# Neighbourhood attention and a feed-forward block: the feed-forward part's seams laid anew, with sums of the down weights kept in DRAM

## The chip, the cores and the metric

The kernel runs on one core of a Trainium2 chip. The metric is the device time of one execution in microseconds (us). A core has TensorE (PE; its weight loads are listed apart as PEld), VectorE (DVE), ScalarE (ACT), GpSimd (POOL) and SyncE (SP), each with its own stream of instructions that it takes in order, and 16 DMA engines, which take transfers from queues that SP, ACT and POOL fill. SBUF is the on-chip memory, PSUM the banks that TensorE writes, DRAM the memory off the core.

## The reference

The input is 1024 prompt rows and 512 sample rows of width 1024, in float32. The reference computes, for one layer:

```
x  = x + attention(rms_norm(x) * norm_mix) @ w_o       # 16 heads, a neighbourhood of rows, a bias table
h  = rms_norm(x) * norm_ffn
x  = x + (silu(h @ w_gate) * (h @ w_up)) @ w_down       # 1024 -> 2816 -> 1024
y  = rms_norm(x) * norm_final
```

All of it is in float32 precision: every matrix operand is split into a high part and the rest, and a product is three matmuls (high x high, high x rest, rest x high).

## The kernel before, in words

The attention part (up to L631) ends with the output projection: `project` (L578) takes an attention row tile and the weights `wo`, 12 matmuls 128x512 at a time into `pgo`, adds x and stores the sum to `x1_d` in DRAM. Only what follows is changed, apart from one early load.

**The operands.** The 1536 rows are worked in two chunks of 768 tokens, each cut into two halves of 384. Each matrix product of the feed-forward part is done on 2x2 blocks with seven products in place of eight (a Strassen-Winograd scheme). Its x side needs seven operands: three blocks and four sums. `norm2` (L658) loads an `x1_d` row tile, normalizes it (square with row sum on ACT, root on POOL, one scalar_tensor_tensor by root and gain on DVE), transposes it in eight 128x128 pieces on PE and copies these from PSUM. `pair` (L672) makes a tile's seven operands from two row tiles. Chunk 0's operands are split into SBUF tiles h0 to h6; chunk 1's go to `hop_d` in DRAM and are reloaded (L812) into the same seven tiles between the chunks. Both chunks' `pair`s stand ahead of the feed-forward part.

**Gate and up.** A chunk has 11 units (`unit`, L786) of 256 columns of the hidden 2816. A unit is a gate block and an up block, and a block (`blocks`) is seven products of 12 matmuls 128x384 into the banks pa, pb and pd. `w_ops` loads the block's two 512 KB halves of weights (`wr`), forms four sums of 128x512 on DVE (L741 to L746), and splits operands (L138 casts on ACT, L139 subtracts on DVE) into `wa` (a single one) and `ws` (two at once). Evacuations into `c` tiles, Silu on ACT, the gate's multiply on DVE, four sums on POOL (`gs`) and seven stores by POOL to `gop_d` follow.

**Down.** The seven operands n are run in the order 0, 1, 4, 5, 2, 6, 3. For each, `d_op` (L839) loads its 11 row pieces of w_d as 256 KB tiles `dr`, forms the sums on POOL (`tk`, L848, L851, L854, and L857) and splits them into `wd`; for each of six token tiles `g_op` (L862) loads 704 KB of `gop_d` into `gr`, splits it into `go`, and 33 matmuls 128x512 fill one of four banks. Additions to x (loaded again from `x1_d` on SP's queue) and, for the last row tiles, the final norm (`finish`, L879) follow each bank. The row tiles' y go out on SP's queue.

**Order.** A scheduler fixes each engine's stream when the kernel is built, from priorities and estimated times, so instructions of neighbouring steps may be interleaved other than written. A tile waits for its memory to be freed by its previous owner. Pools that are closed hand their memory to later ones.

Of the kernel before, what the change touches and what calls it, by code (L numbers as in the profile page):

```python
# [18 lines left out]
P = 128  # L19
D = 1024  # L20
# [35 lines left out]
def body(tc, xp, xs, g_mix, g_ffn, g_fin, w_qkv, rpb, w_o, w_g, w_u, w_d, yp, ys):  # L56
# [9 lines left out]
    with es:  # L66
# [16 lines left out]
        hop_d = dr.tile([7, P, KB // 2, HT], F32, name="hop_d")  # L83
        gop_d = dr.tile([7, 6, P, NP, P], F32, name="gop_d")


        ident = cpool.tile([P, P + 24], F32, name="ident")[:, :P]
# [4 lines left out]
        nc.gpsimd.memset(mhalf, -0.5)  # L92

# [539 lines left out]
        hop_cm, hop = pool("hop", bufs=1, reuse_waits="tile")  # L633

        def h_op(i):
            return hop.tile([P, 2, KB // 2, HT], F32R, tag=f"h{i}", name=f"h{i}")

        def operands(dst, xa, xb, tt):

            b11, b21, b12, b22 = xa[:, :4], xa[:, 4:], xb[:, :4], xb[:, 4:]  # L640
            t1, t2, t3, t4 = (tt[:, n] for n in range(4))
# [12 lines left out]
        n_cm, np_ = pool("npool", bufs=2, reuse_waits="tile")  # L654
        gb = np_.tile([P, D], F32, name="gbf", bufs=1)
        nc.sync.dma_start(out=gb, in_=bcast(g_ffn))

        def norm2(t):  # L658

            xn = np_.tile([P, D], F32, tag="xn", name="xn", bufs=3)  # L660
            nc.scalar.dma_start(out=xn, in_=x1_d[t * P:(t + 1) * P, :])
            xt = np_.tile([P, KB, P], F32, tag="xt", name="xt")
            rms(xn, gb, xn, xt.rearrange("p k t -> p (k t)"))
            for b in range(2):
                pt = psum("T", "pt")
# [3 lines left out]
                nc.scalar.copy(xt[:, b * 4:(b + 1) * 4], pt.rearrange("p (k t) -> p k t", k=4))  # L669
            return xt  # L670

        def pair(c, j, dst):  # L672
            xa = norm2(c * CT + j)
            xb = norm2(c * CT + 3 + j)
            tt = np_.tile([P, 4, KB // 2, P], F32, tag="tt", name="tt", bufs=1)
            operands(dst, xa, xb, tt)

        hops = [h_op(i) for i in range(7)]

        def to_sbuf(j):  # L680
            def dst(i, op):
                split(op, hops[i][:, 0, :, j * P:(j + 1) * P], hops[i][:, 1, :, j * P:(j + 1) * P])
            return dst

        def to_dram(j):
            def dst(i, op):
# [270 lines left out]
```

## Time and profile before

| what | us |
|---|---|
| three runs: lowest, median, highest | 1841.29, 1846.19, 1848.37 |
| the profiled execution's own time | 1845.18 |
| its span | 1843.4 |
| last output-projection matmul ends | 803.3 |
| last gate/up product ends | 1481.6 |
| last down matmul ends | 1835.1 |

The mean granted TensorE clock of the profiled execution is 0.985 of full speed. In the profile's rows a line such as L138 is that of the helper which recorded the operation (a split's cast), so tiles, not lines, tell the groups apart. "Idle before" names what ended an engine's idle time. The DMA share is the mean busy share of the 16 DMA engines.

### The profile page before, as it was taken

How to read it: one execution, taken by the hardware profiler on the slowest of the kernel's cores; microseconds unless marked ns; L12 is line 12 of the kernel's file. 1: busy time of each engine (PE TensorE's matmuls, PEld its weight loads, DVE VectorE, ACT ScalarE, POOL GpSimd, SP SyncE). 2: the span in 40 equal slices, each digit the busy share in tenths (PEclk: the TensorE clock that was granted, in tenths of full speed). 3: DMA queues.
4: the chain of work that ended last, by engine and by line, in shares of the span. 5: the costliest groups of instructions: out<-in, count | busy, mean ns of one | idle time of the engine just before them, and what ended most of it. 6: DMA issues, size and time to landing. Idle time of an engine off the chain costs nothing.

```text
span 1843.4 us, 25648 instructions
## 1 busy us (share of the span) xinstructions
PE 1754.1 (95%) x9178; PEld 1522.5 (83%) x9178; DVE 1192.9 (65%) x2191; ACT 863.7 (47%) x1706; POOL 448.4 (24%) x495
## 2 busy tenths in 40 slices
PE   8999999999999999979999999999999969999898
PEld 6877777777767777868999999899999958887676
DVE  4401877777896566768777777867777444545654
ACT  4411776766785554544443444444443333333322
POOL 1211000000130000112243342424243323526420
PEclk9999999999999999988999999999999979999999
DMA  7755334333464443676343434544333277635732
GB/s 245 221 183 160 111 105 113 108 101 103 126 208 146 133 149 100 221 247 185 108 121 118 133 110 151 164 129 125 108 120 107 68 272 245 225 130 191 232 129 100
DMA packets 222048, 278.80 MB, mean 151 GB/s; under 512 B 25600, under 2 KB 171776, under 8 KB 221920
## 3 DMA queue, kind: packets, MB, share of 16 engines
q1 hardware_dynamic: 201824, 210.69, 37.3%
q0 software_dynamic: 18368, 60.18, 9.5%
q10 hardware_dynamic: 1728, 6.29, 1.1%
q8 instruction: 72, 1.18, 0.3%
q14 instruction: 56, 0.46, 0.1%
HBM read 213.20 MB, written 76.43 MB: 157 GB/s over the span
## 4 chain that ended last, share of the span: by engine, by line
PE 68%; DVE 10%; DMA 9%; ACT 5%; issue 3%; SPq 2%; POOL 2%; DVEq 0%; ACTq 0%; POOLq 0%
PE pa L754 20%; PE pd L910 12%; PE pd L754 10%; PE pgv L278 7%; PE pg L332 6%; PE pb L754 5%; DMA vr<-v_d 5%; PE pgo L586 3%; DMA dr<-ffn_w_down 2%; PE pss L394 2%; PE ptt L420 2%; DVE pT L424 2%; SPq L378 2%; PE po L431 2%; ACT s L405 1%
## 5 line engine op out<-in xcount | busy, mean ns | idle before, releaser
L910 PE MATMUL pd<-wd,go 128*128 128x512 f32 x1386 | 323.0, 395 | 30.5 <-ACT go L138 20.4
L910 PEld LDWEIGHTS pd<-wd,go 128*128 128x128 f32 x1386 | 263.0, 191 | 90.4 <-ACT go L138 21.6
L754 PE MATMUL pa<-h,ws 128*128 128x384 f32 x1056 | 201.8, 339 | 2.9 <-ACT c L777 2.1
L754 PE MATMUL pa<-h,wa 128*128 128x384 f32 x1056 | 195.1, 338 | 7.0 <-ACT wa L138 4.5
L754 PE MATMUL pd<-h,ws 128*128 128x384 f32 x1056 | 198.3, 335 | 1.2 <-ACT h L138 0.6
L332 PE MATMUL pg<-hTp,whl 128*128 128x512 f32 x768 | 193.7, 399 | 0.0
L754 PEld LDWEIGHTS pa<-h,wa 128*128 128x128 f32 x1056 | 185.8, 190 | 8.9 <-ACT wa L138 5.2
L139 DVE TENSOR_TENSOR ws<-wt,ws 128x1024 fp32r<-128x1024 f32 x88 | 108.6, 1235 | 127.1 <-ACT ws L138 126.7
L754 PEld LDWEIGHTS pa<-h,ws 128*128 128x128 f32 x1056 | 185.1, 189 | 6.7 <-ACT c L777 4.3
L754 PEld LDWEIGHTS pd<-h,ws 128*128 128x128 f32 x1056 | 184.5, 188 | 1.8 <-ACT h L138 1.0
L332 PEld LDWEIGHTS pg<-hTp,whl 128*128 128x128 f32 x768 | 139.9, 188 | 27.5 <-issue 0.4
L805 POOL DMA_DIRECT2D gop_d<-c x66 | 50.5, 765 | 387.4 <-DVE c L796 380.3
L405 ACT ACTIVATE s<-s,mx 128x384 f32<-128x384 f32 (+1 forms) x192 | 110.7, 580 | 67.3 <-DVE mx L402 67.1
L586 PE MATMUL pgo<-wo,oh 128*128 128x512 f32 x576 | 139.3, 392 | 0.2 <-DVE oh L139 0.2
L139 DVE TENSOR_TENSOR wa<-wr,wa 128x512 fp32r<-128x512 f32 x132 | 117.8, 897 | 18.4 <-ACT wa L138 17.8
L138 ACT CAST ws<-wt 128x1024 fp32r<-128x1024 f32 x88 | 92.6, 1053 | 68.6 <-PE pd L754 65.4
L586 PEld LDWEIGHTS pgo<-wo,oh 128*128 128x128 f32 x576 | 105.6, 188 | 20.7 <-DVE oh L139 0.6
L138 ACT CAST go<-gr 128x1408 fp32r<-128x1408 f32 x42 | 57.7, 1374 | 131.2 <-PE pd L910 114.0
L138 ACT CAST wa<-wr 128x512 fp32r<-128x512 f32 x132 | 81.4, 621 | 62.8 <-PE pb L754 40.0
L754 PE MATMUL pb<-h,wa 128*128 128x384 f32 x528 | 102.0, 340 | 3.4 <-DVE c L774 3.4
L332 PE MATMUL pg<-hTs,whl 128*128 128x512 f32 x384 | 102.6, 404 | 0.8 <-DVE q L343 0.8
L424 DVE TENSOR_TENSOR pT<-ptt,pT 128x384 fp32r<-128x384 f32 (+1 forms) x192 | 90.0, 507 | 17.3 <-ACT pT L423 16.5
(138 smaller groups left out, 2859.6 us busy)
## 6 DMA issues: line engine op xcount, KB each, us to landing
gr<-gop_d SPq DMA_DIRECT2D x42, 704.0 KB
dr<-ffn_w_down SPq DMA_DIRECT2D x99, 256.0 KB
wr<-ffn_w_gate SPq DMA_DIRECT2D x44, 512.0 KB
wr<-ffn_w_up SPq DMA_DIRECT2D x44, 512.0 KB
wr<-na_w_qkv SPq DMA_DIRECT2D x38, 512.0 KB
gop_d<-gs POOLq DMA_DIRECT2D x88, 192.0 KB, 4.4
gop_d<-c POOLq DMA_DIRECT2D x66, 192.0 KB, 2.8
vr<-v_d SPq DMA_DIRECT2D x192, 64.0 KB
```

The source lines that it names most:

```text
L138: nc.scalar.copy(hi, raw)
L139: nc.vector.tensor_tensor(lo, raw, f32(hi), ALU.subtract)
L278: nc.tensor.matmul(pg, hh[a][:, k, c:c + P], wv[k // 2][b][:, k % 2], start=(k == 0 and i == 0), stop=(k == KB - 1 and i == 2))
L332: nc.tensor.matmul(pg, w[:, a, k, :], h[b][:, k, c:c + 512], start=(k == 0 and i == 0), stop=(k == KB - 1 and i == 2))
L378: nc.sync.dma_start(out=raw[:, j * P:(j + 1) * P], in_=src[:, BS[j]:BS[j] + 32, :])
L394: nc.tensor.matmul(pt[:, :n], q[h * HD:(h + 1) * HD, a, j].rearrange("p r i -> p (r i)"), kv[:, krow:krow + nrow, BS[j]:BS[j] + 32], start ...
L405: nc.scalar.activation(s[:, :n], s[:, :n], AF.Exp, bias=mx, scale=-1.0, accum_out=sm)
L424: nc.vector.tensor_tensor(pT[:, :n, 1], pv, f32(pT[:, :n, 0]), ALU.subtract)
L586: nc.tensor.matmul(pg, ohs[k // 4][:, a, k % 4], wo[:, b, k, n * 512:(n + 1) * 512], start=(k == 0 and i == 0), stop=(k == KB - 1 and i == 2))
L754: nc.tensor.matmul(bank[:, :HT], a(y, k), b[:, z, k], start=start and k == 0 and i == 0, stop=k == KB // 2 - 1 and i == 2, skip_group_chec ...
L805: nc.gpsimd.dma_start(out=gop_d[i, 3 * c:3 * c + 3, :, p].rearrange("j q t -> q j t"), in_=a.rearrange("q (j t) -> q j t", j=3))
L910: nc.tensor.matmul(pd, go[:, y, i], wds[i][:, z], start=(i == 0 and m == 0), stop=(i == NP - 1 and m == 2))
```

## The change

It has six parts.

1. The feed-forward gain `norm_ffn` is loaded at the very start, transposed, as a [128, 8] tile `gT` (1024 pieces of four bytes), the first transfer on SP's queue. `norm2` multiplies by the root alone on ACT, and the gain enters in the copy from PSUM, now a DVE multiplication.
2. Chunk 1's `pair`s become a generator, `pair1`, of which one piece is advanced after every second product (`ticks`) from unit 1 of chunk 0 on. Its temporaries are four 512 KB tiles t0 to t3 in a pool of their own. The rings of split weights shrink: `wa` from 6 to 2 (plus 2 for the last operand), `ws` and `wt` from 3 to 2.
3. Reloads of chunk 1's operands (`reload`) go one at a time into the tile of the operand used before it; the first goes to an extra tile `hx`. The last unit of chunk 0 and the first and last of chunk 1 run their gate and up products interleaved (three products apart).
4. In chunk 1, `down_sums` loads all rows of w_d (22 x 512 KB) into t0 to t3, forms the four sums per pair of row tiles in place, two on DVE and two on POOL, and stores them (22 x 512 KB) to `wt_d` in DRAM.
5. The down stage loads weights and sums as they are (77 pieces of 256 KB, 11 for each of the seven operands, take the place of 99 loads and 44 POOL sums), one piece per half token tile, an operand ahead, with 22 `wd` tiles; g rows come in halves of 384 and 320 KB (three raw, four split buffers). The first tiles are given memory that is freed before the last product. x loads and the first halves' y stores move from SP's queue to POOL's.
6. Squares of the final norm are taken when a half is complete. For the last row tiles the second half of y is multiplied on ACT and stored by ACT's queue.

```diff
+        gT = cpool.tile([P, KB], F32, name="gT")
+        nc.sync.dma_start(out=gT, in_=g_ffn.rearrange("(k p) -> p k", p=P))
...
+            nc.scalar.mul(xn, xn, rs)
+            yield
             for b in range(2):
...
-                nc.scalar.copy(xt[:, b * 4:(b + 1) * 4], pt.rearrange("p (k t) -> p k t", k=4))
+                nc.vector.tensor_tensor(xt[:, ks], pt.rearrange("p (k t) -> p k t", k=4),
+                                        gT[:, ks].rearrange("p (k o) -> p k o", o=1).to_broadcast([P, 4, P]),
+                                        ALU.mult)
...
+        def down_sums():
+
+            def load(i):
+                x, y = temp(2 * (i % 2)), temp(2 * (i % 2) + 1)
+                nc.sync.dma_start(out=x, in_=w_d[2 * i * P:(2 * i + 1) * P, :])
+                nc.sync.dma_start(out=y, in_=w_d[(2 * i + 1) * P:(2 * i + 2) * P, :])
+                return x, y
+
+            rows = load(0)
+            for i in range(NP):
+                yield
+                x, y = rows
+                rows = load(i + 1) if i + 1 < NP else None
+                b11, b12, b21, b22 = x[:, :512], x[:, 512:], y[:, :512], y[:, 512:]
+                nc.vector.tensor_tensor(b11, b12, b11, ALU.subtract)
+                yield
+                nc.vector.tensor_tensor(b12, b22, b12, ALU.subtract)
+                yield
+                nc.sync.dma_start(out=wt_d[0][i * P:(i + 1) * P, :], in_=x)
+                nc.gpsimd.tensor_tensor(b22, b22, b11, ALU.subtract)
+                yield
+                nc.gpsimd.tensor_tensor(b21, b21, b22, ALU.subtract)
+                yield
+                nc.sync.dma_start(out=wt_d[1][i * P:(i + 1) * P, :], in_=y)
...
+        def unit(c, p, hops, tick, after=None):
+
+            gs, us = [], []
+            g, u = blocks(w_g, p, hops, gs), blocks(w_u, p, hops, us)
+            order = [0] * 7 + [1] * 7
+            if after:
+                order = [0] * LAG + [x for _ in range(7 - LAG) for x in (1, 0)] + [1] * LAG
...
+        def reload(n):
+
+            i = ORDER[n]
+            o = h_op(n - 1) if n else h_op("x", hx)
+            for k in range(0, KB // 2, 2):
+                r = temp((2 * n + k // 2) % 4)[:, :2 * HT].rearrange("p (k t) -> p k t", k=2)
+                nc.sync.dma_start(out=r, in_=hop_d[i, :, k:k + 2])
+                hi, lo = o[:, 0, k:k + 2], o[:, 1, k:k + 2]
+                nc.scalar.copy(hi, r)
+                (nc.gpsimd if n in (2, 4) else nc.vector).tensor_tensor(lo, r, f32(hi), ALU.subtract)
+            hops2[i] = o
...
+        pairs = (x for j in range(3) for x in pair1(j))
+        tick = ticks(pairs)
+        for p in range(NP - 1):
+            unit(0, p, hops, tick if p else idle)
+            if p == NP - 2:
+                for _ in pairs:
+                    pass
+                reload(0)
+        unit(0, NP - 1, hops, idle, lambda n: reload(n) if n < 7 else None)
+        sums = down_sums()
+        tick = ticks(sums)
...
+        SRC = {0: (w_d, 0, 0), 1: (w_d, 1, 0), 2: (w_d, 1, 1), 4: (wt_d[0], None, 0), 6: (wt_d[0], None, 1),
+               3: (wt_d[1], None, 0), 5: (wt_d[1], None, 1)}
...
+        for q in range(84):
+            m, tt, h = q // 12, q % 12 // 2, q % 2
+            n = SEQ[m]
+            g_load(q + 3)
+            g_split(q + 2)
+            if q % 12 < NP:
+                d_load(m + 1, q % 12)
+            if q % 12:
+                d_split(m + 1, q % 12 - 1)
...
-            nc.sync.dma_start(out=x, in_=x1_d[t * P:(t + 1) * P, d * 512:(d + 1) * 512])
+            nc.gpsimd.dma_start(out=x, in_=x1_d[t * P:(t + 1) * P, d * 512:(d + 1) * 512])
```

The order of instructions at three places. First PE, from the last output-projection matmuls (`pgo`) on; `pt` are transposes of chunk 1, pa, pb and pd the products' banks. Before:

```order
L586 MATMUL pgo<-wo,oh 128x512 x94
L668 MATMUL pt<-ident,xn 128x128 x16
L754 MATMUL pa<-h_8412,wa 128x384 x9
L668 MATMUL pt<-ident,xn 128x128 x8
L754 MATMUL pa<-h_8412,wa 128x384 x3
L754 MATMUL pb<-h_8413,wa 128x384 x12
L668 MATMUL pt<-ident,xn 128x128 x8
L754 MATMUL pd<-h_8416,ws 128x384 x12
```

and after the change:

```order
L589 MATMUL pgo<-wo,oh 128x512 x88
L814 MATMUL pa<-h_8414,wa 128x384 x12
L814 MATMUL pb<-h_8415,wa 128x384 x12
L814 MATMUL pa<-h_8414,wa 128x384 x2
L814 MATMUL pa<-h_8416,ws 128x384 x2
L814 MATMUL pd<-h_8417,ws 128x384 x2
L814 MATMUL pa<-h_8414,wa 128x384 x4
```

No transposes stand between the first products any more. Second POOL in chunk 1, where the new sums (`t<-t`) stand between the gate sums (`gs`) and the stores of a unit:

```order
L763 TENSOR_TENSOR t_12916<-t_12916,t_12915 128x512
L765 TENSOR_TENSOR t_12916<-t_12916 128x512
L763 TENSOR_TENSOR t_13106<-t_13106,t_13105 128x512
L765 TENSOR_TENSOR t_13106<-t_13106 128x512
L763 TENSOR_TENSOR t_13328<-t_13328,t_13327 128x512
L765 TENSOR_TENSOR t_13328<-t_13328 128x512
L886 DMA gop_d<-c 128x3x128 x2
L881 TENSOR_TENSOR gs<-c 128x384
L882 TENSOR_TENSOR gs<-gs,c 128x384
L883 TENSOR_TENSOR gs<-c 128x384
```

Before, the stores of one unit were followed at once by the sums of the next. Third SP's queue where the down stage begins, after the last weights of the last unit (`wr`). Before:

```order
L714 DMA wr<-ffn_w_up 128x4x256 x2
L829 DMA gff<-norm_final 128x1024
L834 DMA dr<-ffn_w_down 128x512 x11
L864 DMA gr<-gop_d 128x1408
L876 DMA c<-x_d 128x512
L864 DMA gr<-gop_d 128x1408
```

and after the change:

```order
L774 DMA wr<-ffn_w_up 128x4x256 x2
L996 DMA gr<-gop_d 128x768
L981 DMA dr<-ffn_w_down 128x512 x2
L996 DMA gr<-gop_d 128x640
L981 DMA dr<-ffn_w_down 128x512 x2
L996 DMA gr<-gop_d 128x768
L981 DMA dr<-ffn_w_down 128x512 x7
L996 DMA gr<-gop_d 128x640
```

The g rows, in halves, now stand ahead of most row pieces, the gain of the last norm is loaded by ACT's queue, and the x loads are gone from this queue.

More of the change, by code (lines that the diff above doesn't have):

```diff
@@ new lines, in ticks, with tick, idle @@
+        def ticks(work):
+            count = [0]
+            def tick():
+                count[0] += 1
+                if count[0] % 2 == 0:
+                    next(work, None)
+            return tick
+        def idle():
+            pass
+        pairs = (x for j in range(3) for x in pair1(j))
[4 more added lines that the diff above has]
+                for _ in pairs:
+                    pass
+                reload(0)
```

362 lines of the change are left out of this document (213 added, 149 removed).

## The prediction

> **What bounds the kernel now.** I read the page first, then busy time by stretches of the span, then the chain of waits at each place where TensorE stands idle. Times are us.
>
> ```profile
> span 1843.4 us, 25648 instructions
> PE 1754.1 (95%) x9178; PEld 1522.5 (83%) x9178; DVE 1192.9 (65%) x2191; ACT 863.7 (47%) x1706; POOL 448.4 (24%) x495
> ```
>
> TensorE is busy 95% of the span, so a change can win only where it idles or where its granted clock falls. The next rows (start:end, length, busy time and count by engine, clock, DMA share, GB/s) cut up the feed-forward part.
>
> ```profile
> 803.00:850.00 47.00, 33.31 (x153) 30.37 (x152) 32.48 (x49) 23.13 (x39) 3.69 (x5) 0.75 0.90 279
> 850.00:1150.00 300.00, 300.00 (x1723) 297.98 (x1722) 224.75 (x295) 129.50 (x214) 106.46 (x111) 1.00 0.40 122
> 1160.00:1165.00 5.00, 2.93 (x17) 2.61 (x16) 5.00 (x7) 3.02 (x6) 4.04 (x5) 1.00 0.77 234
> 1165.00:1170.00 5.00, 3.81 (x20) 3.23 (x20) 3.88 (x7) 1.86 (x3) 0.00 (x0) 1.00 1.03 388
> 1170.00:1175.00 5.00, 3.83 (x20) 3.25 (x20) 3.64 (x6) 3.75 (x6) 0.00 (x0) 1.00 0.25 88
> 1485.00:1495.00 10.00, 0.00 (x0) 0.00 (x0) 5.62 (x8) 5.05 (x10) 3.60 (x5) 0.50 1.03 359
> 1495.00:1505.00 10.00, 5.84 (x13) 4.16 (x14) 5.19 (x6) 3.87 (x4) 0.00 (x0) 0.50 0.92 338
> 1505.00:1835.00 330.00, 317.06 (x1375) 258.83 (x1373) 176.45 (x186) 108.93 (x156) 115.77 (x79) 0.99 0.55 188
> ```
>
> Away from its seams the gate and up stage is saturated: 300 of 300 busy, and 300/1723 = 0.174 per 128x384 matmul. The losses sit at four places, and the chain (start, length, what) says what ended them:
>
> ```profile
> 795.23 8.03 PE pgo L586 x34
> 805.78 7.78 DMA wr<-ffn_w_gate
> 833.43 0.87 PE pt L668 x8
> 1163.34 7.30 DMA hr<-hop_d
> 1479.52 2.10 PE pa L754 x12
> 1483.44 5.56 DMA dr<-ffn_w_down
> 1491.02 6.26 DMA gr<-gop_d
> 1716.03 3.65 DMA dr<-ffn_w_down
> 1741.68 2.40 POOL tk L848
> 1760.48 68.65 PE pd L910 x302
> ```
>
> *Seam 1*, from the last output-projection matmul (795.23 + 8.03 = 803.26) to 850: of the 153 matmuls, 48 are transposes at 0.87/8 = 0.11 (5.2) and 105 cost 0.174 (18.3), so 46.7 - 23.5 = 23.2 is lost, part idle, part at a lower clock. *Seam 2*, 1160 to 1175: 15 - 10.57 = 4.4 idle at clock 1.00. *Seam 3*: the last product ends at 1481.62; up to 1505 are 23.4, in which 13 down matmuls ran, worth 13 x 68.65/302 = 3.0, so 20.4 is lost. *Inside the down stage*: the other 1373 of its 1386 matmuls need 1373 x 0.2273 = 312.1 of the 330.1 up to 1835.1; 18.0 is lost, with loads and POOL sums of down rows in the chain. Together 66.
>
> **The change part by part.** *Seam 1.* Chunk 1's loads, norms and operands leave it; their 48 transposes stay, scattered among later products. In the new order the last projection matmuls are followed by the first product, whose weights lie in a buffer already loaded, and then by the second, whose half of the rows goes into memory that the projection's weights hold until its last matmul. So a 512 KB load starts there. It costs between 7.78, above, and the first x load, alone on the queue (the chain's row):
>
> ```profile
> 0.74 4.36 DMA x<-x_prompt
> ```
>
> With a cast and a subtraction (about 0.62 and 0.69) behind the load and 2.1 of products over it, the gap is 3.6 to 7.0; the next sums and splits add 1 to 3, and the clock may fall. I take 8 (5 to 14): **-15.2**. The clock did fall to 0.50 in seam 3's idle 10 and stayed 1.00 in seam 2's gaps of a few us. [...]
>
> Chunk 1's preparation now runs under units 1 to 7 of chunk 0: per pair of tiles two norms, four PSUM evacuations and four 0.69 sums, about 6 of DVE, 18 in all. The cover is DVE's idle quarter (224.75 busy of 300); a stalled piece has several products of slack in the order. Cost 0.
>
> *Seam 2.* Reloads of chunk 1's operands go one slot behind the products that free them, and the units on both sides interleave gate and up. What is left is a weight ring of two; I take 0.7 (0 to 4): **-3.7**.
>
> *The sums.* In chunk 1, 22 DVE and 22 POOL sums of 128x512 and 44 transfers of 512 KB are new; the order puts them in about its first 107. Rows of the timeline (start, length, engine, line, what) and the stretch:
>
> ```profile
> 1257.62 1.23 DVE L139 TENSOR_TENSOR ws<-wt,ws 128x1024 fp32r<-128x1024 f32 x1 [2.09 <-ACT ws L138]
> 1262.80 0.69 DVE L745 TENSOR_TENSOR wt<-wr 128x512 f32<-128x512 f32 x1
> 1250.12 1.50 DVE L745 TENSOR_TENSOR wt<-wr 128x512 f32<-128x512 f32 x1
> 1266.44 2.24 PE L754 MATMUL pa<-h,ws 128*128 128x384 f32 x12
> 1252.45 1.46 POOL L803 TENSOR_TENSOR gs<-c,gs 128x384 f32<-128x384 f32 x1
> 1200.00:1307.00 107.00, 107.00 (x617) 106.55 (x616) 78.06 (x106) 44.67 (x73) 33.00 (x35) 1.00 0.39 117
> ```
>
> DVE has 78 of 107 busy. The new work is 22 x 0.69 = 15, and each POOL sum that meets a DVE sum of two SBUF tiles lengthens it by 1.50 - 0.69 = 0.81, at most 22 x 0.81 = 18: demand 93 to 111 of 107, while split weights lie ready about 7 before use (the 1.23 split ends at 1258.85, its product starts at 1266.44). The transfers add 23 MB, 215 GB/s to 117; 388 was moved in seam 2. Bounds 0 (cover holds) and 16 (worked below under the slower rival); I take 3, near the covered end since the sums and the surplus over 107 are within the slack: **+3**.
>
> *Seam 3.* The first tiles now lie over memory freed before the last product: the first half of the g rows over the extra operand slot, free once the last unit's up block has used it (ten products of 2.08 before the end), the second half about three products (6.2) before the end. The other down rows stand behind this second half on SP's queue, so some 2 MB start at -6.2 and, at 359 GB/s, are there by about -0.6. Eleven splits at about 0.7 then feed a bank that PE takes in 7.5. I take 5 (2 to 10): **-15.4**.
>
> *Inside the down stage.* 44 POOL sums and 22 of 99 row loads go away, each bank's row pieces come one per half tile, twice as many weight tiles are held, so the switch of operand is prepared through the six banks before it. Per half tile 0.6 MB moves in 3.75, 165 GB/s, less than the 188 above. POOL's 44 sums (two of their four groups below: busy time, mean ns, idle before and its releaser) took about 1.6 each, 71; in their place it issues the 24 x loads and 12 of the y stores that stood on SP's queue, at the 0.77 of its other stores 28, and each stands in line with its remaining sums and roots.
>
> ```profile
> L848 POOL TENSOR_TENSOR tk<-dr,tk 128x512 f32<-128x512 f32 x11 | 19.7, 1811 | 12.4 <-DMA dr<-ffn_w_down 12.4
> L851 POOL TENSOR_TENSOR tk<-dr 128x512 f32<-128x512 f32 x11 | 17.6, 1613 | 9.4 <-DMA dr<-ffn_w_down 9.4
> L805 POOL DMA_DIRECT2D gop_d<-gs x88 | 67.3, 767 | 0.1
> ```
>
> Left over are the first banks and the fifth operand, where roots wait behind x loads; 3 (1 to 8): **-15.0**.
>
> *Tail and start.*
>
> ```profile
> 1835.16 0.69 DVE L896 TENSOR_TENSOR u<-u,pd 128x512 f32<-128x512 f32 x1 [3.03 <-PE pd L910]
> 1836.56 0.61 ACT L884 ACTIVATE yo<-c 128x512 f32<-128x512 f32 x1
> 1837.08 0.19 ACT L884 ACTIVATION_READ_ACCUMULATOR yo<-c 128x1 f32 x1
> 1838.91 0.75 DVE L892 SCALAR_TENSOR_TENSOR yo<-c,rs,gff 128x512 f32<-128x512 f32 x1
> q1 hardware_dynamic: 201824, 210.69, 37.3%
> ```
>
> One square (0.8) and one of two products in a row (0.7) leave the end: **-1.5**. In front, the transposed gain vector is the first transfer: 1024 pieces of four bytes, 64 on each of 16 engines. The queue's packets took 0.373 x 1843.4 x 16/201824 = 0.0545 each, so 3.5, and x stands behind it on the queue. Bounds: 1 (pieces overlap) and 5 (with a slower issue); I take **+3**.
>
> Sum: -15.2 - 3.7 + 3 - 15.4 - 15.0 - 1.5 + 3 = -44.8. The profiled execution took 1845.2, 1.0 below the median of 1846.2: 1800.4 for it, **1801** for a median.
>
> **The rivals.** *A: DVE is locked out in chunk 1* (faster, 1810). If each POOL sum shuts out DVE sums for all of its 1.46 instead of adding 0.81, demand is 78 + 15 + 32 = 125 in 107, 18 over; less the slack of 7, 11 to 12 instead of 3. For it: 1.50 against 0.69. Against: the wider products on PSUM aren't touched, and scheduled POOL work meets DVE's pauses too. [...]
>
> *B: a seam stays* (the change doesn't do what it says; 1824). The second half of g or the row loads land 10 late and seam 1 keeps 15 to 20 because its first loads still wait for the projection: 12 + 10 of gain lost. For it: the same waits on PE stand in the new order. Against: what is queued behind them is far less than the 90% DMA share of 803 to 850.
>
> *C: the POOL queue holds the down stage* (1813). In the fifth operand six adds wait for x rows (256 KB, about 3.65 as for the down rows) in front of six square roots: 6 x 3.65 = 22, of which four banks of PSUM cover part; some 12 more.
>
> *D: the sums' round trip paces chunk 1* (slower, 1862). Two sets of buffers turn over 11 times. A turn is a load, two DVE sums, two POOL sums, a store: 7.8 + 1.4 + 2.9 + 7.8 = 20 at seam 1's price, and 5.5 turns fill the 107 exactly. Behind a waiting sum on POOL stand the unit's four gate sums and seven stores, and behind these the c tiles that the next unit's evacuations need. At 24 a turn it costs 5.5 x 4 = 22, less about 7 of slack: 15. It turns slower than before from 20 + (47.8 + 7)/5.5 = 30 a turn; at 33 it costs 5.5 x 13 - 7 = 64: 1845.2 - 47.8 + 64 + 1 = 1862. Against: that needs transfers of 14 to 15, twice the worst above, at 332 GB/s in all.
>
> **How the numbers follow.** Chances: forecast 0.48, A 0.15, B 0.14, C 0.11, D 0.07, and 0.05 that several of them meet at no change. About 0.5% is what a measurement of this kernel tells from no change. The first four are faster by more: faster 0.88, same 0.05, slower 0.07. The low end takes every term's good bound (3 + 0.7 + 3 + 3 + 2 + 2 = 13.7 less): 1787. The high end holds B with another term at its bad bound: 1827.
>
> **What would show it.** Right: no idle over 8 after the last projection matmul; PE full from then through chunk 1 at 0.174 a matmul; DVE at 85 to 100% in its first 107; first down matmul within 5 of the last product; under 4 idle in the down stage. Wrong: granted clock 0.5 for 10 or more at a seam; PE gaps ended by a split behind a POOL sum or a row load (A, D); POOL ended by loads of x (C); a first x load that lands past 9 instead of 5.1 (the start).

## The result, and the profile after

The change made the kernel faster by less than a third of what was forecast: 1831.66 us (median of 4 runs, 1830.81 to 1833.53) against 1845.89 for the kernel before on the same chip, a ratio of 0.9921 with a 95% interval of 0.9899 to 0.9943. Forecast were 1801 and a range of 1787 to 1827; the time lies outside it. The profiled execution took 1832.42. Its page (span, and busy time by engine):

```profile
span 1830.6 us, 25932 instructions
PE 1759.3 (96%) x9178; PEld 1524.8 (83%) x9178; DVE 1222.3 (67%) x2263; ACT 874.8 (48%) x1742; POOL 439.9 (24%) x513
```

TensorE ran the same 9178 matmuls and was busy 5.2 longer than before. To see where, I cut the span at the forecast's own places. First the rows of the gate and up products alone (start:end, length, PE, PEld, clock, DMA share, GB/s):

```profile
803.00:850.00 47.00, 42.37 (x224) 41.38 (x224) 0.93 0.48 148
890.00:1000.00 110.00, 101.25 (x548) 98.82 (x547) 0.95 0.47 149
1127.00:1167.00 40.00, 36.78 (x209) 35.82 (x208) 1.00 0.73 233
1167.00:1272.00 105.00, 93.47 (x508) 90.59 (x507) 0.97 0.86 294
```

Then the transposes in the second of these stretches, and the down products:

```profile
890.00:1000.00 110.00, 3.59 (x24) 2.99 (x24) 0.95 0.47 149
...
1460.00:1505.00 45.00, 7.22 (x23) 5.11 (x24) 0.96 0.46 154
1505.00:1825.00 320.00, 317.62 (x1365) 255.63 (x1363) 1.00 0.56 184
```

What is lost in each is its length less what its matmuls need, at the prediction's 0.174 for a product, 0.2273 for a down matmul and 0.11 for a transpose. Seam 1: 47 - 224 x 0.174 = 8.0. Chunk 0: 110 - 548 x 0.174 - 24 x 0.11 = 12.0. Seam 2: 40 - 209 x 0.174 = 3.6. Sums: 105 - 508 x 0.174 = 16.6. The chain gives the ends of the attention part and of the last product (start, length), and the timeline the end of the last down matmul:

```profile
783.18 19.99 PE pgo L589 x88
...
1491.84 2.12 PE pa L814 x12
```

```profile
1814.63 8.51 PE L1058 MATMUL pd<-wd,go 128*128 128x512 f32 x36
```

The last product ends at 1493.96, so seam 3 is 1505 - 1493.96 - 23 x 0.2273 = 5.8. The other 1363 down matmuls fill 1505 to 1823.1, 318.1, where 309.8 were needed: 8.3.

| place | lost before | left by forecast | lost after |
|---|---|---|---|
| seam 1 | 23.2 | 8 | 8.0 |
| chunk 0, 890 to 1000 | 0 | 0 | 12.0 |
| seam 2 | 4.4 | 0.7 | 3.6 |
| the sums, 1167 to 1272 | 0 | 3 | 16.6 |
| seam 3 | 20.4 | 5 | 5.8 |
| inside the down stage | 18.0 | 3 | 8.3 |
| sum | 66.0 | 19.7 | 54.3 |

With 0.8 gained behind the last down matmul that makes 12.5; the spans differ by 12.8. The attention part ends where it did: 783.18 + 19.99 = 803.17, before 803.26. Two new losses, 28.6 together, ate what the seams gave, and a third place kept 8.3 although TensorE hardly waits there (one stop of 0.50 after 1505), as the next sections show.

### The profile page after: what moved, and what is told of

Same layout as the page of the kernel before. It is cut to its first block, busy times and chain, and to the rows that moved or that the text cites. A ratio compares the mean times of both kernels' runs of the same rounds, so it can differ in the third digit from the quotient of the medians.

```text
span 1830.6 us, 25932 instructions
## 1 busy us (share of the span) xinstructions
PE 1759.3 (96%) x9178; PEld 1524.8 (83%) x9178; DVE 1222.3 (67%) x2263; ACT 874.8 (48%) x1742; POOL 439.9 (24%) x513
## 4 chain that ended last, share of the span: by engine, by line
PE 63%; DVE 13%; DMA 10%; ACT 6%; issue 3%; POOL 2%; SPq 2%; POOLq 0%; DVEq 0%; ACTq 0%
PE pd L1058 15%; PE pa L814 15%; PE pd L814 7%; PE pgv L281 6%; PE pg L335 5%; DMA vr<-v_d 5%; PE pgo L589 4%; PE pb L814 4%; DVE pT L427 2%; SPq L381 2%; PE pss L397 1%; PE ptt L423 1%; ACT s L408 1%; PE po L434 1%; DVE oT L447 1%
## 5 line engine op out<-in xcount | busy, mean ns | idle before, releaser
L814 PE MATMUL pa<-h,ws 128*128 128x384 f32 x1056 | 205.8, 344 | 15.2 <-ACT c L839 11.1
L814 PEld LDWEIGHTS pa<-h,ws 128*128 128x128 f32 x1056 | 189.5, 194 | 18.7 <-ACT c L839 12.8
L142 DVE TENSOR_TENSOR ws<-wt,ws 128x1024 fp32r<-128x1024 f32 x88 | 114.7, 1305 | 97.5 <-ACT ws L141 97.4
L814 PE MATMUL pa<-h,wa 128*128 128x384 f32 x792 | 148.1, 338 | 7.2 <-DVE c L846 7.0
L814 PEld LDWEIGHTS pa<-h,wa 128*128 128x128 f32 x792 | 139.3, 188 | 9.2 <-DVE c L846 8.6
L141 ACT CAST go<-gr 128x768 fp32r<-128x768 f32 x84 | 65.6, 781 | 151.3 <-PE pd L1058 113.1
L142 DVE TENSOR_TENSOR wa<-wr,wa 128x512 fp32r<-128x512 f32 x132 | 124.4, 954 | 10.2 <-ACT wa L141 9.1
L142 DVE TENSOR_TENSOR go<-gr,go 128x768 fp32r<-128x768 f32 x84 | 81.6, 974 | 73.0 <-ACT go L141 71.7
```

Of the source, the lines that this page charges most:

```text
L141: nc.scalar.copy(hi, raw)
L142: nc.vector.tensor_tensor(lo, raw, f32(hi), ALU.subtract)
L814: nc.tensor.matmul(bank[:, :HT], a(y, k), b[:, z, k], start=start and k == 0 and i == 0, stop=k == KB // 2 - 1 and i == 2, skip_group_chec ...
```

## What the new losses look like

**Chunk 0.** The timeline of three engines around one of the stops (start, length, engine, line, what, in brackets the idle time ahead and what ended it). POOL first, then ACT, then PE:

```profile
903.90 1.46 POOL L883 TENSOR_TENSOR gs<-c 128x384 f32<-128x384 f32 x1
905.32 1.46 POOL L884 TENSOR_TENSOR gs<-c,gs 128x384 f32<-128x384 f32 x1
906.73 0.77 POOL L886 DMA_DIRECT2D gop_d<-c  x1
907.49 3.05 POOL L886 DMA_DIRECT2D gop_d<-gs  x4
910.56 0.57 POOL L673 TENSOR_TENSOR rs<-me,mhalf 128x1 f32<-128x1 f32 x1
```

```profile
911.16 1.15 ACT L675 ACTIVATE t<-t,rs 128x1024 f32<-128x1024 f32 x1 [2.80 <-POOL rs L673]
912.22 0.46 ACT L839 COPY c<-pa 128x384 f32<-128x384 f32 x1
```

```profile
912.73 1.65 PE L814 MATMUL pa<-h,ws 128*128 128x384 f32 x4 [3.71 <-ACT c L839]
```

A root of one column stands on POOL behind the four gate sums and the stores of a unit. The multiplication by it is next in ACT's stream: ACT stands idle for 2.80, then multiplies for 1.15, and the copy that empties a product's bank comes only then, at 912.22, although the product's last matmul ended at 906.94. TensorE stops for 3.71, and its clock dips (0.95 over the stretch). A second stop of the same kind, of 3.90, ends at 979.77; the two make 7.6 of the 12.0, and the rest, 4.4, goes with the lower clock. TensorE and ACT stand still while POOL issues its stores; a cover counted in busy time does not show it.

**The sums.** All engines from 1167 to 1272 (PE, PEld, DVE, ACT, POOL), then DVE's groups there (busy time, mean ns):

```profile
1167.00:1272.00 105.00, 93.47 (x508) 90.59 (x507) 98.36 (x108) 34.95 (x60) 67.40 (x53) 0.97 0.86 294
```

```profile
L142 DVE TENSOR_TENSOR ws<-wt,ws 128x1024 fp32r<-128x1024 f32 x13 | 20.2, 1551 | 0.6 <-ACT ws L141 0.6
L760 DVE TENSOR_TENSOR t<-t,t 128x512 f32<-128x512 f32 x11 | 13.2, 1206 | 0.4 <-DMA t<-ffn_w_down 0.4
L758 DVE TENSOR_TENSOR t<-t 128x512 f32<-128x512 f32 x10 | 6.8, 683 | 5.5 <-issue 3.0 <-DMA t<-ffn_w_down 2.6
```

DVE is busy 98.36 of 105: it is the bound here, and it waits little, mostly in front of sums whose rows are loaded (L758). Of the two DVE sums of a row pair, priced at 0.69 each, one takes 1.21 on average and the other 0.68, and the splits of pairs take 1.55 instead of 1.23.

**The down stage.** In its middle, DVE's additions from successive banks show the pace (start, length), before and after:

```profile
1812.72 0.69 DVE L896 TENSOR_TENSOR u<-u,pd 128x512 f32<-128x512 f32 x1 [2.13 <-PE pd L910]
1820.20 0.69 DVE L896 TENSOR_TENSOR u<-u,pd 128x512 f32<-128x512 f32 x1 [2.13 <-PE pd L910]
```

```profile
1784.94 0.69 DVE L1030 TENSOR_TENSOR u<-u,pd 128x512 f32<-128x512 f32 x1 [1.63 <-PE pd L1058]
1792.59 0.69 DVE L1030 TENSOR_TENSOR u<-u,pd 128x512 f32<-128x512 f32 x1 [1.67 <-PE pd L1058]
```

A bank of 33 matmuls took 7.48 and now takes 7.65, with DVE waiting for PE and not the other way round, at a granted clock of 1.00. 0.17 x 42 banks is 7.1 of the 8.3.

## The experiments

Kernels that ran together share a chip, and the kernel before read 1843.8 to 1846.2 on these chips; so the ratios to it (in brackets the 95% interval) are the firm numbers. Differences in us are between medians, against 1831.66 and 0.9921 of the change.

**The sums: is it their work, and is it POOL?** The first kernel leaves the sums, their loads and their stores out and runs all seven operands on rows of w_d, so that its four sum operands are not the reference's.

```diff
-        sums = down_sums()
+        sums = iter(())
...
```

> The changed kernel without the sums of the down weights: no loads, sums or stores of them in chunk 1, and the down stage reads plain rows of w_d in place of the stored sums, in as many loads of the same size (so four of the seven down operands are not the reference's). Theory: in the 105 us in which the sums run, DVE is busy 98.4 and TensorE makes 508 of 603 matmuls; all of this loss of 16.5 is the sums', so the time is 1815 (1813 to 1818), with DVE at 74% there. Rival: the loss belongs to the interleaved first unit and its reloads, which stay; then 1825 to 1830.

Measured: 1814.56, ratio 0.9839 [0.9816, 0.9862]: 17.1 less. A stretch inside the same place (all engines), of the change and without the sums:

```profile
1200.00:1250.00 50.00, 46.56 (x255) 45.93 (x256) 46.34 (x51) 19.36 (x34) 29.98 (x24) 0.97 0.87 296
```

```profile
1200.00:1250.00 50.00, 50.00 (x289) 49.93 (x288) 36.91 (x49) 19.76 (x33) 17.39 (x18) 1.00 0.31 99
```

TensorE is full again. The sums cost all that is lost there. The second kernel keeps each piece of them behind the instruction that DVE or POOL was given before it, so that the eleven groups spread over some eight units; the third does this and puts the two POOL sums on DVE.

```diff
+                    for e in engines:
+                        new = [i for i in traced[mark:] if i.engine == e.engine]
+                        old = next((i for i in reversed(traced[:mark]) if i.engine == e.engine), None)
+                        for b in new[:1]:
+                            tc.add_manual_dep(b, old.name, mybir.DependencyInfo(
+                                mybir.DependencyClass.NoSync, mybir.DependencyReason.DATA), reason="pin")
...
-        tick = ticks(sums)
+        tick = ticks(sums, (nc.vector, nc.gpsimd))
```

> The changed kernel with the same sums held to their places in the text: each DVE and POOL piece may not be scheduled ahead of the product that it is written behind, so 11 groups spread over some eight units (230 us) in place of 105. Theory: the loss is DVE's demand above the time in the packed stretch; spread, DVE needs about 75% + 33/230 = 89% and no product waits: 1817 (1815 to 1821). Rival: each POOL sum or each late load stops DVE's queue in front of a split that TensorE needs, however far apart they are; then 11 groups keep most of their price, 1826 to 1832.

Measured: 1823.12, 0.9885 [0.9861, 0.991]: 8.5 back, between the theory's range and the rival's. What is left are stops of 0.25 to 1.36. One of the meetings that cause them, from the timeline of this kernel, DVE and POOL, with a split of the same shape that met nothing:

```profile
1285.48 2.38 DVE L142 TENSOR_TENSOR ws<-wt,ws 128x1024 fp32r<-128x1024 f32 x1 [0.96 <-ACT ws L141]
1290.66 1.22 DVE L142 TENSOR_TENSOR ws<-wt,ws 128x1024 fp32r<-128x1024 f32 x1
```

```profile
1285.47 1.30 POOL L763 TENSOR_TENSOR t<-t,t 128x512 f32<-128x512 f32 x1
```

Beside a POOL sum of 1.30 the DVE split takes 1.16 longer: nearly the POOL sum's whole length is added, not a part of it.

```diff
-                nc.gpsimd.tensor_tensor(b22, b22, b11, ALU.subtract)
+                nc.vector.tensor_tensor(b22, b22, b11, ALU.subtract)
...
-                nc.gpsimd.tensor_tensor(b21, b21, b22, ALU.subtract)
+                nc.vector.tensor_tensor(b21, b21, b22, ALU.subtract)
```

> The spread sums (1823.1, measured with two of the four sums of a row pair on POOL) with all four on DVE. Theory: a POOL sum costs DVE its whole length (a split of 1.22 took 2.38 beside a POOL sum of 1.30), so 22 of them cost DVE 22 x 1.2 = 26, more than the 22 x 0.69 = 15 of doing them itself: the stops of 0.3 to 1.4 after 1200 go and the time is 1819 (1817 to 1822). Rival: DVE's own demand counts, and 15 more of it makes it worse: 1825 to 1830.

Measured: 1817.1, 0.9848 [0.9827, 0.9869]: 14.6 of the 16.6 back. So the bunching of the work and the POOL sums beside it are the cause; the transfers, which are all still made, cost little. How the two share it is less sure. The medians say 8.5 and 6.0, with overlapping intervals. The profiled executions say something else: from 1167 to 1460 the change ran 1586 products, the spread sums 1643, those on DVE 1656, and the kernel without the sums 1682. At 0.174 each, spreading gave 9.9 back there and the move to DVE 2.3.

**The stops in chunk 0.** Here the multiplication by the root stands three steps (six products) later, and the pieces' ACT instructions are kept behind those given before them.

```diff
-            yield
+            for _ in range(4):
+                yield
             nc.scalar.mul(xn, xn, rs)
...
-        tick = ticks(pairs)
+        tick = ticks(pairs, (nc.scalar,))
```

> The changed kernel (1831.7) with one thing different in chunk 0: the ACT multiplication by the root comes six products later in the text than the POOL root it needs, and ACT's scheduler may not hoist it ahead. Theory: the 12 us lost between 890 and 1000 are two stops of some 6 each, in which ACT's in-order queue waits for a root that stands on POOL behind a unit's four sums and seven stores, with a PSUM copy behind it that TensorE needs. Then both stops go, the stretch runs at 0.174 a matmul, and the time is 1820 (1817 to 1823). Rival: the added DVE and DMA work of the pieces is what slows chunk 0; then the stops stay somewhere and the time is 1829 to 1832.

Measured: 1826.22, 0.9901 [0.9877, 0.9925]: 5.4 back, though the intervals overlap, and less than the theory said. The two large stops are gone; smaller ones (0.3 to 3.1) are left, and since the pieces come later, the last of them run into the reloads: from 1100 to 1150 only 227 products ran, where the change had 278, (278 - 227) x 0.174 = 8.9 lost. The next kernel starts the preparation a unit earlier, with one step less of delay.

```diff
-            unit(0, p, hops, tick if p else idle)
+            unit(0, p, hops, tick)
...
```

> The changed kernel with chunk 1's pieces begun one unit earlier and the ACT multiplication held four products behind the POOL root in place of none (the run with six and no earlier beginning gave 1826.2: its two stops of 6 were gone, but the last pieces came so late that the reload lost 9 between 1100 and 1150, where the changed kernel lost 1). Theory: both are gone then: 1819 to 1822. Rival: the delayed pieces keep a cost of their own wherever they end; 1825 to 1829.

Measured: 1829.16, 0.9912 [0.9891, 0.9933], no gain that can be told from the change: a miss. The wait had only moved. In ACT's timeline a square now stands in front of the copies and waits for its row tile:

```profile
979.96 1.06 ACT L669 ACTIVATE t<-t 128x1024 f32<-128x1024 f32 x1 [5.62 <-DMA t<-x_d]
```

The third one spaces every step from what it needs: both loads, three steps, the squares, three steps, the multiplications, then transposes and sums.

```diff
...
+            for st in steps:
+                next(st)
+            for _ in range(3):
+                yield
+            for st in steps:
+                next(st)
+                yield
...
```

> The changed kernel (1831.7) with chunk 1's pieces begun one unit earlier and arranged per pair: both loads, three steps (of two products each) of nothing, both squares, three steps, both multiplications, then transposes and sums, two steps before the next pair's loads, each ACT piece held to its place in the text. Theory: every stop in chunk 0, also the smaller ones of the two earlier tries (0.3 to 3.1, ended by ACT copies behind a square that waits for its rows or a multiplication that waits for its root), is an ACT piece that waits in front of a PSUM copy; with both waits given time, no stop over 0.5 stays between 850 and 1100 and the time is 1820 (1818 to 1823). Rival: the pieces' own ACT and DVE time (1.1 to 1.2 in front of a copy) is enough to stop TensorE; then stops of about 1 stay, 1825 to 1829.

Measured: 1824.09, 0.9883 [0.9868, 0.9898]: 7.6 back, just above the theory's range. From 890 to 1000 there ran 613 products and 16 transposes, where the change had 548 and 24, and the clock held (products alone):

```profile
890.00:1000.00 110.00, 107.84 (x613) 105.91 (x611) 1.00 0.46 143
```

No copy stands behind a waiting square or multiplication any more. Three stops of 0.97 to 1.13 stay, and they are not those of the rival. Two follow a Silu that waits on ACT for a DVE addition (3.67 and 3.53), which stands behind two splits that take 1.4 to 1.5 each beside POOL's gate sums, in place of 0.68. The third follows a cast of the first reload that waits 2.99 for its load. So ACT's order was the cause of the two large stops; but a piece must be spaced for each of its inputs, not for the one last seen to be late.

**Seam 2.** The first unit of chunk 1 runs its gate before its up, as all others do.

```diff
-                order = [0] * LAG + [x for _ in range(7 - LAG) for x in (1, 0)] + [1] * LAG
+                order = [0] * LAG + [x for _ in range(7 - LAG) for x in (1, 0)] + [1] * LAG if c == 0 or p else [0] * 7 + [1] * 7
```

> The changed kernel with the first unit of chunk 1 not interleaved (seven gate products, then seven up products, as in all middle units); the last units stay interleaved. Theory: interleaving is what gives the reloads time, since a reloaded operand (two casts on ACT, two subtractions of 0.92 on DVE, two loads) is needed every 4.2 in place of every 2.1; without it TensorE waits for operands as it did before the change: 1834 (1832 to 1837). Rival: the interleaved unit's loss of 3.6 between 1127 and 1167 comes from the preparation of two weight blocks at once; without it 1828 to 1830.

Measured: 1828.23, 0.9904 [0.9887, 0.9921]. The theory's 1834 did not come. It is 3.4 less in the medians, with overlapping intervals, but the gain is not in the seam: from 1127 to 1167 this kernel ran 204 products, where the change ran 209, and from 1167 to 1272, under the sums, 526 where the change ran 508. The largest stop of the seam, 2.76, is there in both. DVE, POOL and PE of the changed kernel ahead of it:

```profile
1145.90 2.36 DVE L806 TENSOR_TENSOR wt<-wr,wt 128x512 f32<-128x512 f32 x1
1148.19 2.86 DVE L142 TENSOR_TENSOR ws<-wt,ws 128x1024 fp32r<-128x1024 f32 x1
1151.57 0.54 DVE L846 TENSOR_TENSOR c<-c,pa 128x384 f32<-128x384 f32 x1
1145.88 4.09 POOL L900 TENSOR_TENSOR h<-t,h 128x768 fp32r<-128x768 f32 x2 [5.13 <-ACT h L899]
1152.16 2.38 PE L814 MATMUL pa<-h,wa 128*128 128x384 f32 x12 [2.76 <-DVE c L846]
```

Two of the seven reloads have their subtractions on POOL. Beside them a DVE sum of 0.69 takes 2.36 and a split of 1.22 takes 2.86, and the addition that empties the bank (L846) stands behind both. It looks like the loss of the sums in small; but this is read from order and times, and no run takes these subtractions off POOL.

**The pace of the down matmuls.** My first theory was that PE waits in the middle of a bank, where the second half of the g rows is split; with whole g tiles the pace should return.

```diff
-            return rt.tile([P, 2, 6, P], F32R, tag=f"go{n}", name="go")
+            return rt.tile([P, 2, NP, P], F32R, tag=f"go{n}", name="go")
```

> The changed kernel with the g rows of the down stage in whole tiles of 704 KB (two raw, two split buffers) in place of halves (three raw, four split). Theory: a bank of 33 matmuls takes 7.65 in place of the 7.48 of the kernel before because a second weight tile is waited for in its middle; with whole tiles it is 7.48 again, 42 x 0.17 = 7 less, and the beginning of the down stage is up to 3 worse: 1826 (1824 to 1829). Rival: the slower bank comes from something else in the new down stage (the loads, the 22 weight tiles, POOL's transfers); then the bank stays at 7.65 and the time is 1831 to 1836.

Measured: 1838.17, 0.996 [0.995, 0.9971], 6.5 worse by a slower beginning of the down stage (from 1505 to 1600 it ran 378 matmuls, the change 406), and the pace stayed at 7.64:

```profile
1790.27 0.69 DVE L1028 TENSOR_TENSOR u<-u,pd 128x512 f32<-128x512 f32 x1 [3.97 <-PE pd L1056]
1797.91 0.69 DVE L1028 TENSOR_TENSOR u<-u,pd 128x512 f32<-128x512 f32 x1 [2.95 <-PE pd L1056]
```

The theory fell. What else differs is where the tiles lie (all starts below are those that the built programs give). On the left side the change starts 128 bytes lower after the small tiles, since the four `ms2` tiles of the old final norm are gone; `ident` gave up the 32 bytes that the gain tile takes. The pools of the down stage are new on both sides. Padding `ident`, a constant that nothing reads past column 128, shifts the left side of SBUF by 128 bytes, then by 256, and does nothing else.

```diff
-        ident = cpool.tile([P, P + 16], F32, name="ident")[:, :P]
+        ident = cpool.tile([P, P + 48], F32, name="ident")[:, :P]
```

> The changed kernel (1831.7) with 128 bytes per partition of unused space more at the start of on-chip memory, so that everything on its left side lies 128 bytes further. Theory: a matmul of 512 columns takes 6.7 ns more when one of its two operands starts at a multiple of 512 bytes; the change moved 19 of 22 weight tiles of the down stage there (a bank 7.65 to 7.70, before 7.48) and moved the v weights of the attention part away from it (a bank of 24 5.44, before 5.60). With 128 more both are as before: down banks 7.48, 42 x 0.19 = 8 less, v banks 5.60, 16 x 0.16 = 2.6 more: 1826 (1824 to 1828). Rival: the slower bank comes from the side of memory, or from the new order of loads; then banks stay at 7.65 and 5.44 and the time is 1831 to 1833.

> The same with 256 bytes more: then neither the v weights, nor the transposed rows, nor the down weights start at a multiple of 512. Theory: down banks 7.48, v banks 5.44 throughout (in the changed kernel 5.57 for the sample rows): 1831.7 - 8 - 1 = 1823 (1821 to 1825). If it is multiples of 256 that cost, the down banks stay at 7.65 and the time at 1831; by the rival too.

Measured: with 128 bytes 1824.3, 0.9886 [0.9864, 0.9907] and 7.48 a bank; with 256 bytes 1832.12, 0.9922 [0.9896, 0.9948] and 7.64. With 128:

```profile
1791.90 0.69 DVE L1030 TENSOR_TENSOR u<-u,pd 128x512 f32<-128x512 f32 x1 [1.57 <-PE pd L1058]
1799.38 0.69 DVE L1030 TENSOR_TENSOR u<-u,pd 128x512 f32<-128x512 f32 x1 [1.57 <-PE pd L1058]
```

So the loss is one of addresses: a shift of 128 bytes took it away, and one of 256 left it as it was. The two operands of a down matmul lie on both sides of SBUF: in the kernel before both started at 128 modulo 256, in the changed one mostly at 0 and 128. But the v projection shows the same in reverse. Its banks (ACT's copies of them, before and after) took 5.60 and now take 5.44, and 5.57 again with the pad:

```profile
101.44 0.59 ACT L281 COPY vs<-pgv 128x512 f32<-128x512 f32 x1 [5.01 <-PE pgv L278]
107.04 0.59 ACT L281 COPY vs<-pgv 128x512 f32<-128x512 f32 x1 [5.01 <-PE pgv L278]
```

```profile
102.10 0.59 ACT L284 COPY vs<-pgv 128x512 f32<-128x512 f32 x1 [4.87 <-PE pgv L281]
107.54 0.59 ACT L284 COPY vs<-pgv 128x512 f32<-128x512 f32 x1 [4.85 <-PE pgv L281]
```

Two theories fit: both operands must start at 128, or both must start alike. The first kernel below aligns v and down at 128 (the pad, and 128 bytes more in front of the v weights). The second leaves the left side as it is and shifts the right side by 128, so that down meets at 0 and 0.

```diff
-            fill = vp.tile([P, 480], F32, tag="fill", name="fill", bufs=1)
+            fill = vp.tile([P, 512], F32, tag="fill", name="fill", bufs=1)[:, :480]
```

> The changed kernel (1831.7) with 128 bytes of unused space at the start of on-chip memory and 128 more ahead of the v weights, so that both operands of all 512-column matmuls start 128 bytes past a multiple of 256. Theory (address): v banks 5.44 throughout, q and k banks 5.44, down banks 7.48: 1831.7 - 8 - 2 = 1822 (1820 to 1824), 2 to 3 below the 1824.3 of 128 bytes alone. Rival: the v stage's 2.6 are hidden behind its loads; then 1824.

```diff
-        edge = es.enter_context(tc.tile_pool(name="edge", bufs=1, side="right")).tile([P, 24], F32, name="edge")
+        edge = es.enter_context(tc.tile_pool(name="edge", bufs=1, side="right")).tile([P, 56], F32, name="edge")[:, :24]
```

> The changed kernel with the right side of on-chip memory shifted by 128 bytes: g rows and weight tiles of the down stage both start at multiples of 256, and so do the q and k stage's operands and the output projection's. If operands must only start alike, down banks are 7.48 and q and k banks 5.44 (1824). If each must start 128 bytes past a multiple, both operands are wrong everywhere: down banks 7.65 or more, q and k banks 5.57 or more (1832 to 1850).

Measured: 1820.38, 0.9867 [0.9849, 0.9884], with v 5.44 and down 7.48; and 1819.35, 0.9861 [0.9846, 0.9875], with down 7.48 at 0 and 0 and v 5.57:

```profile
1794.98 0.69 DVE L1030 TENSOR_TENSOR u<-u,pd 128x512 f32<-128x512 f32 x1 [1.57 <-PE pd L1058]
1802.46 0.69 DVE L1030 TENSOR_TENSOR u<-u,pd 128x512 f32<-128x512 f32 x1 [4.29 <-PE pd L1058]
```

Of the two theories alike is the one that fits; the q and k banks agree, 5.44 at 128 and 128 as at 0 and 0, and 5.57 in the change at 128 and 0. By the medians the two kernels are worth 11.3 and 12.3. The pad alone gave 7.4, about down's 7.1; but a shift of one side moves all that lies there, so with the pad v's banks were slower and q's and k's quicker, and no sum is split up cleanly between the stages.

**Together.** Three kernels join what helped. The first (paced preparation, sums on DVE, and `ident` padded by 64 bytes, from a wrong guess at the rule) came before the address runs were done:

> Three changes at once: the paced pieces of chunk 1, the four sums of a row pair on DVE and spread over eight units, and 64 bytes of unused space at the start of on-chip memory, with which no operand of a matmul starts at a multiple of 256. If what the single runs showed adds up: 1831.7 - 11 (paced) - 14.6 (the sums on DVE, spread: 1817.1) - 8 - 1 (down banks 7.48, v banks of the sample rows 5.44) = 1797 (1795 to 1802). If they share a cover (DVE) or the 64 bytes are not enough: 1803 to 1815.

Measured: 1818.18, 0.9851 [0.9836, 0.9866]. It missed: at 64 bytes the starts stay unlike (64 and 128), and down ran at 7.66. Not every unlike pair cost the same: v's banks took 5.49 at 192 and 128, q's and k's 5.50 at 128 and 64.

> The changed kernel with the four sums of a row pair on DVE and spread over eight units (1817.1 alone) and the full alignment of e12. If they add up: 1817.1 - 10 = 1807 (1805 to 1811). If the sums' DVE work and the weights' come together in the shorter time: up to 1814.

> The same with the paced pieces of chunk 1 (1824.1 alone, 7.6 less than the changed kernel). If it adds up: 1807 - 7.6 = 1799 (1797 to 1804). With 64 bytes in place of 128 and 128 these three gave 1818.2, where the address rule says 1817.1 - 7.6 + 4 for the attention part = 1813; if the difference of 5 is a cost of pacing together with spread sums, 1804 to 1808.

Measured: sums spread on DVE with both alignments, 1809.42, 0.9809 [0.9794, 0.9824]; with the paced preparation as well, 1801.63 (1800.87 to 1804.86), 0.9769 [0.9753, 0.9785]. This one beats both kernels: 30.0 less than the change in the medians, where the parts alone gave 14.6 + 11.3 + 7.6 = 33.5. Its page and two of its stretches:

```profile
span 1800.3 us, 25936 instructions
PE 1742.8 (97%) x9178; PEld 1517.1 (84%) x9178; DVE 1213.0 (67%) x2285; ACT 875.4 (49%) x1742; POOL 408.7 (23%) x491
```

```profile
850.00:1100.00 250.00, 246.88 (x1433) 244.73 (x1432) 194.04 (x263) 110.77 (x181) 90.97 (x92) 1.00 0.50 156
...
1150.00:1460.00 310.00, 307.00 (x1758) 304.13 (x1757) 249.31 (x336) 124.80 (x208) 116.49 (x119) 1.00 0.57 185
```

Same matmuls, same new transfers, TensorE busy 99% in both stretches, once the three causes are out. That the time also meets the forecast's 1801 is in part luck: small losses such as the stop at seam 2 stay, and the aligned v banks (5.44, in the kernel before 5.60) are a gain that the forecast did not have; the attention part ended 1.4 earlier, at 801.8.

## Why the prediction was wrong, step by step

The direction was right, and so were two of the three largest terms. **Seam 1** was to leave 8 and left 8.0: one stop of 4.41 in front of the second product, whose weights come late as forecast, and most of the rest at a clock of 0.93. With bounds of 5 to 14, the exact hit is luck. **Seam 3** was to leave 5 and left 5.8. The waits **inside the down stage** went as said. The tail gave 0.8 of 1.5. Four steps failed, together 33.8 too hopeful; the start, which cost hardly anything of its 3, less what seam 3 and the tail fell short, takes 1.5 of it back.

1. "Chunk 1's preparation now runs under units 1 to 7 of chunk 0 ... The cover is DVE's idle quarter ... Cost 0." It cost 12.0, in two stops of 3.71 and 3.90 and the lower clock around them. The step asked which engine has busy time to spare, and none lacked it. It did not ask what each moved instruction waits for and what stands behind it in its stream: root behind POOL's stores, multiplication behind the root, bank copy behind the multiplication. The same prediction did ask this of POOL in rival D. The order of ACT and POOL at this place would have shown it.
2. "The sums ... I take 3": 16.6, just past the upper bound of 16. The step let each POOL sum add 0.81 to a DVE sum and took the surplus as covered by a slack of 7. What the runs show is rival A's case: beside a POOL sum of 1.30 a DVE split of 1.22 took 2.38, longer by nearly the whole POOL sum. A found 18 too much for the 107 and took the slack of 7 off, 11 to 12; what was lost is near the 18. With the sums in a bunch and DVE busy 98.36 of 105, the slack was used up. Spreading alone gave half of it back. Rival D's part, the round trip of the buffers, was not seen: DVE waited some 6 in the stretch for its loads at most.
3. "Inside the down stage ... Left over ... 3": 8.3. Little of it is the waits that the step named. About 0.17 a bank, 7.1 in all, is a slower matmul, from operands whose starts no longer agree modulo 256 bytes. No term could hold this: the rate of an unchanged instruction was taken over from the profile before.
4. "Seam 2 ... I take 0.7": 3.6, within its own bounds (0 to 4). The step left a weight ring of two as the only cost. What the trace shows is a stop of 2.76 behind DVE work that was drawn out beside the reloads' subtractions on POOL (a sum from 0.69 to 2.36, a split from 1.22 to 2.86). Running the first unit without interleaving left this stop as it was; that the subtractions on POOL are its cause is not tested.

The **start** was put at +3, from 64 pieces of 0.0545 one behind the other. It cost about 0.3 at the first transposes and 0.6 at the first v matmuls, before and after:

```profile
8.10 1.94 PE L129 MATMUL pt<-ident,xn 128*128 128x128 f32 x8 [8.10 <-DVE xn L122]
8.42 1.94 PE L132 MATMUL pt<-ident,xn 128*128 128x128 f32 x8 [8.42 <-DVE xn L125]
```

The 3.5 that the pieces would take one behind the other did not show. By the end of the attention part nothing of it is left (803.17 against 803.26), where the v banks got faster and the q and k banks slower. Rival B (a seam stays) and C (POOL's queue holds the down stage) were not seen: the seams left 8.0 and 5.8, and after 1505 TensorE waited 0.50 up to the last matmul.

The range was too narrow. Its low end took every term's good bound; its high end did not take every bad one, which would have been 34.3 more than 1801, 1835. Two terms were set at their covered end, and the 0 for chunk 1's preparation had no bounds at all.

## What to carry to other kernels

Chunk 1's preparation, moved under other work, cost 12.0 here: ACT stood idle for 2.80 in front of a multiplication whose root was late, and TensorE stopped for 3.71 behind it. Spaced for each of its inputs, the same work gave 7.6 back. So follow, on each engine, what the moved piece waits for and which evacuation of PSUM stands behind it, and space the pieces for each input. Count busy time as cover only over the stretch where the order really puts the work, and count a POOL sum of two SBUF tiles on DVE as well, where DVE too reads two of them: here a DVE split took 1.16 longer beside a POOL sum of 1.30, and the spread sums were 6.0 faster by the medians with all four on DVE. After any change of tiles, compare the pace of an untouched, unstalled stage first: if it has moved, as the down banks did here from 7.48 to 7.65, look at where the operands start.

## What the runs showed of the hardware

In these runs a matmul of 128x512 took about 2 to 7 ns more (0.17 to 0.22 of 33, 0.05 to 0.16 of 24) when the starts of its two operands in SBUF differed modulo 256 bytes. Moving and stationary operand, modulo 256, as the built programs place them, and the time of a bank in the traces:

| starts | down, 33 matmuls | v, 24 matmuls | q and k, 24 matmuls |
|---|---|---|---|
| 128, 128 | 7.48 (before, e5_pad128, e12_aligned) | 5.44 (the change, e12_aligned) | 5.44 (before, e5_pad128, e12_aligned) |
| 0, 0 | 7.48 (e13_equal0) | - | 5.44 (e13_equal0) |
| 0, 128 | 7.65 to 7.70 (the change, e6_pad256) | 5.57 to 5.60 (e5_pad128, before) | - |
| 128, 0 | - | 5.57 (the change, sample rows) | 5.57 (the change) |
| 64, 128 | 7.66 (e10_best) | - | - |
| 192, 128 | - | 5.49 (e10_best) | - |
| 128, 64 | - | - | 5.50 (e10_best) |

Which mechanism is behind it stays open; the table says only that like starts were the fast ones here, at 0 as at 128, and that unlike ones cost between about a third (5.49 against 5.44) and all (5.60) of the difference.

In the changed kernel the granted clock was 0.93 over 803 to 850, with a stop of 4.41, 0.95 over 890 to 1000, with stops of 3.71 and 3.90, and 0.97 over 1167 to 1272, with one of 3.27. A stop of about 2.75 at seam 2 went both ways: in the changed kernel the clock was 1.00 from 1147 to 1167, around the stop of 2.76; in the kernels without the sums and with spread sums, whose longest stops before the down stage from 1150 on were 2.7 and 2.8, it was 0.97 from 1150 to 1200.
